# One kernel, one change: the depthwise convolution's work shared out anew in the first stage of a hybrid decoder trunk

## The chip, the cores and the metric

The kernel runs on one core of a Trainium2 chip. A core has five engines that run at the same time and in order, each from its own queue: TensorE (PE, matrix products, which write to a memory of eight banks called PSUM), VectorE (DVE), ScalarE (ACT), GpSimd (POOL) and SyncE (SP). SP and ACT also issue the DMA transfers here. The metric is the time of one execution on the device, in microseconds, and the median of several runs is compared. A profile comes from one further execution; its span runs from the first instruction to the last.

## The reference

Two layers on x of 512 tokens by 1024 channels, all in float32. Only the first half of the first layer is touched by the change:

```python
def conformer_conv(x, w_pw1, b_pw1, w_dw, b_dw, ln_g, ln_b, w_pw2, b_pw2):
    a = jax.nn.glu(x @ w_pw1 + b_pw1, axis=-1)
    y = lax.conv_general_dilated(          # causal, depthwise, 31 taps
        a, w_dw[:, None, :], window_strides=(1,),
        padding=((CONV_WIDTH - 1, 0),),
        dimension_numbers=('NWC', 'WIO', 'NWC'),
        feature_group_count=D_MODEL) + b_dw
    y = jax.nn.silu(layernorm(y, ln_g, ln_b))
    return y @ w_pw2 + b_pw2

h = h + conformer_conv(rmsnorm(h, norm_mix[0]), ...)
h = h + swiglu_ffn(rmsnorm(h, norm_ffn[0]), ffn_w_up[0], ffn_w_down[0])
# then: shared K/V, banded attention with a relative-position bias table,
# a second feed-forward part, and a final RMSNorm
```

## The kernel before

**Layout.** Activations lie with channels on the 128 partitions and the 512 tokens along the free axis, so the 1024 channels are eight tiles (ct = 0 to 7). Each float32 operand of a large product is split in a high part and a low rest (names `whi`, `wlo` for weights), and three matmuls (hi·hi, hi·lo, lo·hi) take the place of one. Weights arrive in chunks of 128 x 1024 (`raw`, 512 KB, on SP's queue). `advance` loads six chunks ahead and splits three ahead: a copy on ACT makes `whi`, a subtraction on DVE makes `wlo` (both line 269).

**Start.** x comes in four transfers on SP's queue (L375), the first weight chunk in three pieces on ACT's queue (L373), then on SP's queue the second chunk, `rnd` (a table of convolution weights, L378) and `wdw`. ACT and DVE split the eight tiles of x (each scaled by the norm's gain) and the first two chunks, in an order written out with `Turn`, a helper that puts every operation behind the one before (recorded at line 280). Then come the squares of x, whose sum gives the RMS scale. PE starts on the projection without that scale; the scale is multiplied in when the results are read out of PSUM.

**The RMS scale.** In the middle of tile 1's projection `step1` sums the squares over the partitions on PE. DVE then forms the mean square (L428), POOL takes it to the power -0.5 (L430), DVE writes it on diagonals (L442), and `step2` spreads it over all partitions with one product and a copy on ACT (L437, `rsbc`). Until then no projection result can be read out.

**A tile of the convolution.** `project` makes the linear and the gate half on PE, in an order written out by hand (`in_turn`, line 337). `gate` applies the RMS scale (L758, L760), the sigmoid on ACT (L759) and the product (L761) into `apad`, 512 tokens with 30 zeros in front. Then the 31 taps are shared out:

- *Rounds* on PE. `apad` is written to DRAM (`rowsd`, L766) and read back four times, shifted by one token each (`shifted`, L768), so that 32 channels times 4 shifts fill the partitions. A round applies four taps: four matmuls with 32 output channels each. Their weights, `tables`, are diagonals that DVE makes out of `eye` and `rnd` (L725).
- *Taps* on DVE: one fused multiply-add each (`taps`, recorded at 280), accumulated in a PSUM bank.
- *Products* on ACT (L803, L806) with the additions on POOL (L808, and L821 into y).
- On the last tile alone, four taps as full diagonal products on PE.

`ROUNDS`, `N_DIAG` and `N_DVE` set the shares; what remains goes to the products. `last` adds the rounds' bank to `y[ct]` (L825). The rounds of tile ct stand on PE inside the projection of tile ct + 2; those of tiles 4 to 7 stand behind all projections.

**LayerNorm.** `shift_rows` takes a common offset off y (two products with ones, L837). `sums` adds up y and y² for pairs of tiles on PE, in one bank. After the last tile `scales` copies that bank out, forms mean and variance per token, takes the power on POOL, and spreads both over the partitions (`pm`, `prs`). Then each tile is made: subtract, multiply (DVE), Silu (ACT, L935), a copy for the high part (L936) and a subtraction for the low part. They feed `pw2`, the second product.

**The bias table.** `table` makes one row of bias per head, `f1`. `table_rows` copies it in four transfers to 128 rows of DRAM (`fd`, L671), and `read_bias` reads it back along a diagonal, in eight transfers of two heads each (L957), during the second product; the attention needs it later.

`tc.issue_after` fixes that one instruction is put behind another; where nothing fixes it, the program's scheduler chooses the order on each engine. `held` gives the instructions behind which weight splits are put.

Of the kernel before, what the change touches and what calls it, by code (L numbers as in the profile page):

```python
# [37 lines left out]
ROUNDS = (3, 3, 3, 3, 3, 3, 4, 5)  # L38
N_DIAG = (0, 0, 0, 0, 0, 0, 0, 4)
N_DVE = (9, 9, 9, 9, 9, 9, 7, 4)  # L40
# [132 lines left out]
def hybrid_trunk(ctx: ExitStack, tc: tile.TileContext, xT, W, prm_in, wdw_in, rnd_in, sinks, relb, onehot, fin, out):  # L173
# [203 lines left out]
    rnd = cv.tile([P, ROUND_COLS[-1]], F32, tag="rnd", name="rnd", bufs=1)  # L377
    nc.sync.dma_start(rnd, rnd_in)  # L378
# [23 lines left out]
    class Rms:  # L402
# [16 lines left out]
        def step1(self):  # L419
# [8 lines left out]
            nc.vector.tensor_scalar(ms, st[:, 0:4], 1.0 / D, EPS, op0=ALU.mult, op1=ALU.add)  # L428
            self.rs = small.tile([P, 4], F32, tag="rs", name=uid("rs"))
            nc.gpsimd.tensor_tensor(self.rs, ms, mhalf, op=ALU.pow)  # L430
            self.diag = diagonals(self.rs)
# [212 lines left out]
    with conv_stage:  # L644
        sk = cpool.tile([P, NH], F32, tag="sk", name="sk")
        fd = dpool.tile([P, NH, 3 * P], F32, tag="fd", name="fd")
# [21 lines left out]
        def table_rows(n):  # L668

            rows = slice(n * 32, (n + 1) * 32)  # L670
            nc.sync.dma_start(fd[rows].rearrange("q h k -> q (h k)"), f1.to_broadcast([32, NH * 3 * P]))  # L671
# [12 lines left out]
        sel = cv.tile([P, 2], F32, tag="sel", name="sel", bufs=1)  # L684
# [7 lines left out]
        acts, dves = Turn(), Turn()  # L692
        for k in range(KT):
# [23 lines left out]
        begun = dves.last  # L717
        held[0] = (acts.last, dves.last)
        weights_of = {}
        for ct, r in enumerate(ROUNDS):  # L720
            at = ROUND_COLS[ct]
            t, base = (tables[0], 0) if ct < 5 else (tables[1], ROUND_COLS[5])
            weights_of[ct] = t[:, at - base:at - base + 4 * r, :]
            with tc.issue_after(begun):
                nc.vector.tensor_mul(weights_of[ct], eye.unsqueeze(1).to_broadcast([P, 4 * r, 32]),  # L725
                                     rnd[:, at:at + 4 * r].unsqueeze(2).to_broadcast([P, 4 * r, 32]))
        class Conv:
# [58 lines left out]
            def rounds(self):  # L786
# [3 lines left out]
                for n in range(self.r):  # L790
                    for g in range(4):
# [31 lines left out]
            def last(self):  # L823
                ct = self.ct
                nc.vector.tensor_add(y[ct], self.c, y[ct])  # L825
                if ct in (2, 3):
                    nc.gpsimd.tensor_add(y[ct], y[ct], shift)
# [443 lines left out]
```

## Time and profile before

| | |
|---|---|
| median of 3 runs | 1073.04 us (1072.49 to 1073.49) |
| the profiled execution | 1073.53 us |
| its span | 1071.6 us |
| mean granted PE clock | 0.989 |
| first stage, to the first matmul of the second product | 0 to 166.1 us |
| PE busy in the whole span | 1040.2 us (97%) |
| DVE, ACT, POOL busy | 764.5, 507.2, 199.0 us |

A row of the timeline gives the start and the length in us, the engine, the line, the operation with its output and inputs, and a count; in brackets the idle time of the engine ahead of it and what ended it. Float32 products show two records each, so "x24" at the rounds are twelve matmuls (three rounds). A row of the DMA issues gives the size of one transfer and the median time from issue to landing.

### The profile page before, as it was taken

How to read it: one execution, taken by the hardware profiler on the slowest of the kernel's cores; microseconds unless marked ns; L12 is line 12 of the kernel's file. 1: busy time of each engine (PE TensorE's matmuls, PEld its weight loads, DVE VectorE, ACT ScalarE, POOL GpSimd, SP SyncE). 2: the span in 40 equal slices, each digit the busy share in tenths (PEclk: the TensorE clock that was granted, in tenths of full speed). 3: DMA queues.
4: the chain of work that ended last, by engine and by line, in shares of the span. 5: the costliest groups of instructions: out<-in, count | busy, mean ns of one | idle time of the engine just before them, and what ended most of it. 6: DMA issues, size and time to landing. Idle time of an engine off the chain costs nothing.

```text
span 1071.6 us, 15899 instructions
## 1 busy us (share of the span) xinstructions
PE 1040.2 (97%) x6368; PEld 892.0 (83%) x6368; DVE 764.5 (71%) x988; ACT 507.2 (47%) x774; POOL 199.0 (19%) x209
## 2 busy tenths in 40 slices
PE   8888989999999999999999999999999999999997
PEld 6555727888999899899988777788899988998996
DVE  7869857769786577658576676577978755776663
ACT  6466645534354255235363675454445522552353
POOL 0698950321000000000022333132100000000000
PEclk9898999999999999999999999999999999999999
DMA  6767543324224124321322211232423341343112
GB/s 227 199 196 192 138 133 117 101 89 164 79 99 153 45 90 144 102 80 60 117 81 88 73 57 40 65 95 96 138 80 100 121 154 40 98 138 99 40 60 79
DMA packets 37205, 114.34 MB, mean 107 GB/s; under 512 B 4443, under 2 KB 7436, under 8 KB 37004
## 3 DMA queue, kind: packets, MB, share of 16 engines
q1 hardware_dynamic: 35836, 111.71, 33.3%
q10 hardware_dynamic: 1296, 1.62, 0.4%
q8 instruction: 50, 0.82, 0.3%
q14 instruction: 23, 0.19, 0.1%
HBM read 108.98 MB, written 7.49 MB: 109 GB/s over the span
## 4 chain that ended last, share of the span: by engine, by line
PE 81%; DVE 1%; issue 1%; ACT 1%; POOLq 0%; POOL 0%; ACTq 0%
PE bank L345 23%; PE bank L346 22%; PE bank L347 22%; PE bank L337 12%; PE bank L1200 2%; DVE quad L460 1%; DVE wlo L269 0%; PE bank L1190 0%; PE bank L452 0%; PE bank L426 0%; ACT whi L269 0%; DVE h L489 0%; ACT tmp L935 0%; ACT tmp L607 0%; ACT quad L459 0%
## 5 line engine op out<-in xcount | busy, mean ns | idle before, releaser
L346 PE MATMUL bank<-quad,whi 128*128 128x256 f32 (+1 forms) x1536 | 489.0, 320 | 0.9 <-DVE quad L460 0.9
L345 PE MATMUL bank<-quad,whi 128*128 128x256 f32 (+1 forms) x1536 | 482.9, 320 | 1.8 <-ACT quad L936 1.1
L347 PE MATMUL bank<-quad,wlo 128*128 128x256 f32 (+1 forms) x1536 | 481.9, 319 | 0.0
L269 ACT CAST whi<-raw 128x1024 fp32r<-128x1024 f32 x174 | 182.3, 1050 | 294.6 <-PE bank L346 195.2
L345 PEld LDWEIGHTS bank<-quad,whi 128*128 128x128 f32 x1536 | 291.2, 190 | 24.7 <-ACT quad L936 1.9
L346 PEld LDWEIGHTS bank<-quad,whi 128*128 128x128 f32 x1536 | 292.5, 190 | 22.7 <-DVE quad L460 1.3
L347 PEld LDWEIGHTS bank<-quad,wlo 128*128 128x128 f32 x1536 | 290.0, 190 | 20.6 <-issue 0.5
L269 DVE TENSOR_TENSOR wlo<-raw,whi 128x1024 fp32r<-128x1024 f32 x174 | 225.0, 1296 | 114.3 <-ACT whi L269 105.0
L337 PE MATMUL bank<-quad,whi 128*128 128x512 f32 x512 | 161.9, 397 | 2.4 <-ACT whi L280 2.4
L337 PEld LDWEIGHTS bank<-quad,whi 128*128 128x128 f32 x512 | 95.2, 189 | 29.2 <-issue 6.3
L269 DVE TENSOR_TENSOR wlo<-blocks,whi 128x1024 fp32r<-128x1024 f32 x54 | 65.4, 1221 | 57.0 <-ACT whi L269 57.0
L337 PE MATMUL bank<-quad,wlo 128*128 128x512 f32 x256 | 100.7, 393 | 2.1 <-DVE wlo L269 2.1
L269 ACT CAST whi<-blocks 128x1024 fp32r<-128x1024 f32 x54 | 56.6, 1048 | 91.6 <-PE bank L346 70.0
L808 POOL TENSOR_TENSOR quad<-quad 128x512 f32<-128x512 f32 x63 | 91.1, 1448 | 11.6 <-ACT quad L806 7.9
L337 PEld LDWEIGHTS bank<-quad,wlo 128*128 128x128 f32 x256 | 48.3, 189 | 13.5 <-DVE wlo L269 2.5
L1211 POOL TENSOR_TENSOR rs<-ss,mhalf 128x1 f32<-128x1 f32 x4 | 2.2, 548 | 297.9 <-DVE ss L1209 297.9
L806 ACT ACTIVATE quad<-apad,wdw 128x512 f32<-128x512 f32 x63 | 43.9, 719 | 26.4 <-POOL quad L808 26.2
L416 POOL TENSOR_TENSOR tmp<-tmp,tmp 128x512 f32<-128x512 f32 x21 | 33.0, 1571 | 113.0 <-ACT tmp L414 88.9
L1073 POOL COPY sc<-sk 128x4 f32<-128x4 f32 x16 | 3.5, 253 | 257.0 <-DVE wlo L269 254.8
L1097 POOL TENSOR_SCALAR sc<-sc,sm 128x256 f32<-128x256 f32 (+1 forms) x64 | 31.7, 515 | 67.5 <-DVE sm L1095 67.4
L489 DVE TENSOR_TENSOR h<-bank,h 128x512 f32<-128x512 f32 x56 | 37.1, 683 | 8.2 <-PE bank L347 8.1
L1093 ACT ACTIVATE sc<-sc,m 128x257 f32<-128x257 f32 (+1 forms) x64 | 30.2, 475 | 22.2 <-DVE m L1084 22.2
(158 smaller groups left out, 1007.2 us busy)
## 6 DMA issues: line engine op xcount, KB each, us to landing
raw<-in_W_dram SPq DMA_DIRECT2D x139, 512.0 KB, 3.5
blocks<-in_W_dram SPq DMA_DIRECT2D x36, 512.0 KB, 4.1
shifted<-rowsd SPq DMA_DIRECT2D x24, 260.0 KB, 5.6
fd<-f SPq DMA_DIRECT2D x4, 768.0 KB, 9.7
rowsd<-apad SPq DMA_DIRECT2D x8, 271.0 KB, 2.6
bias<-fd SPq DMA_DIRECT2D x8, 256.0 KB, 5.3
shifted<-rowsd SPq DMA_DIRECT2D x4, 264.0 KB, 5.1
shifted<-rowsd SPq DMA_DIRECT2D x4, 262.0 KB, 4.7
```

The lines of the kernel that those rows point to most:

```text
L269: done = (nc.scalar.copy(hi, r).ins, lo_engine[0].tensor_sub(lo, r, f32(hi)).ins)
L337: turn[0] = nc.tensor.matmul(*args, **kw).ins
L345: nc.tensor.matmul(out, w[0], x[0], start=start, stop=False, **kw)
L346: nc.tensor.matmul(out, w[0], x[1], start=False, stop=False, **kw)
L347: nc.tensor.matmul(out, w[1], x[0], start=False, stop=stop, **kw)
L416: eng.tensor_add(sq, self.acc[eng], sq)
L489: nc.vector.tensor_add(t, banks[m], t)
L806: nc.scalar.mul(pr, src, self.tap(j))
L808: nc.gpsimd.tensor_add(to, acc, pr)
L1093: nc.scalar.activation(sc[:, j, 0:1 + w], sc[:, j, 0:1 + w], AF.Exp, bias=self.m4[:, j:j + 1], scale=-1.0, accum_out=sm[:, j:j + 1])
L1097: nc.gpsimd.tensor_scalar(sc[:, j, 1:1 + w], sc[:, j, 1:1 + w], sm[:, j:j + 1], 0.0, op0=ALU.mult, op1=ALU.add)
L1200: nc.tensor.matmul(self.banks[g], x, w[:, k, :], start=False, stop=kp == LAST[1] - 1 and k == 1 and n == 2)
```

## The change

It has six parts, all in the first stage:

- **Shares.** Tiles 1, 3 and 5 get four rounds for three and eight DVE taps for nine; tile 6 gets eight taps for seven. Products per tile become 10, 7, 10, 7, 10, 7, 7, 3 (before 10 in tiles 0 to 5, then 8 and 3).
- **Order of the first loads.** `rnd` moves to ACT's queue behind the first quarter of the first weight chunk; x, the rest of that chunk and the second chunk go on SP's queue, in the order of use.
- **Tables.** Instead of eight together ahead of the mean square, three are made before all else on DVE, two behind the mean square (beside POOL's power), three behind the diagonals.
- **Bias table.** `fd` has 16 rows, one transfer, behind tile 3's projection; each of the eight reads then writes 16 partitions with all heads.
- **Offset.** `shift_rows` stands half a projection later, behind tile 4's.
- **LayerNorm.** The sums of tiles 4 to 6 and their copy (`means`) come ahead of tile 7's rounds. Tile 7's y is added in its PSUM bank by a product with the identity; its sums are eight products with a column of 1/1024, added onto the same bank. The first tile's high part is written by a Silu of its own.

```diff
-ROUNDS = (3, 3, 3, 3, 3, 3, 4, 5)
+ROUNDS = (3, 4, 3, 4, 3, 4, 4, 5)
-N_DVE = (9, 9, 9, 9, 9, 9, 7, 4)
+N_DVE = (9, 8, 9, 8, 9, 8, 8, 4)
...
-    for a, b in ((0, 256), (256, 512), (512, 1024)):
-        nc.scalar.dma_start(early[0][0][:, a:b], W[0][:, a:b])
-    for a, b in ((0, 1), (1, 2), (2, 4), (4, 8)):
+    nc.scalar.dma_start(early[0][0][:, 0:256], W[0][:, 0:256])
+    nc.scalar.dma_start(rnd, rnd_in)
+    load_x(0, 1)
+    load_x(1, 2)
+    nc.sync.dma_start(early[0][0][:, 256:1024], W[0][:, 256:1024])
+    load_x(2, 4)
     nc.sync.dma_start(early[1][0], W[1])
-    nc.sync.dma_start(rnd, rnd_in)
+    load_x(4, 6)
+    load_x(6, 8)
     nc.sync.dma_start(wdw, wdw_in)
...
             nc.gpsimd.tensor_tensor(self.rs, ms, mhalf, op=ALU.pow)
-            self.diag = diagonals(self.rs)
+            if between is not None:
+                had = between(had)
+            with tc.issue_after(had):
+                self.diag = diagonals(self.rs)
...
-        fd = dpool.tile([P, NH, 3 * P], F32, tag="fd", name="fd")
+        fd = dpool.tile([16, NH, 3 * P], F32, tag="fd", name="fd")
-            nc.sync.dma_start(fd[rows].rearrange("q h k -> q (h k)"), f1.to_broadcast([32, NH * 3 * P]))
+            nc.sync.dma_start(fd.rearrange("q h k -> q (h k)"), f1.to_broadcast([16, NH * 3 * P]))
...
+        def round_weights(cts, after=None):
+            for ct in cts:
+                at, n = ROUND_COLS[ct], 4 * ROUNDS[ct]
+                with tc.issue_after(after) if after is not None else nullcontext():
+                    after = nc.vector.tensor_mul(weights_of[ct], eye.unsqueeze(1).to_broadcast([P, n, 32]),
+                                                 rnd[:, at:at + n].unsqueeze(2).to_broadcast([P, n, 32])).ins
+            return after
+
+        dves.last = round_weights(range(3))
...
+                    if self.n_diag and n == self.r - 1:
+                        in_turn(self.c, ident, y[self.ct], start=False, stop=False, skip_group_check=True)
...
-        def scales():
+        def means():
             sc = temp()
-            with tc.issue_after(nc.scalar.copy(sc, st[0]).ins):
-                nc.scalar.activation(warm, warm, AF.Silu)
+            nc.scalar.copy(sc, st[0])
             b = bank()
             for n in range(NBLK):
-                in_turn(b[:, 2 * n:2 * n + 2], sc[:, n * P:(n + 1) * P], sel, start=True, stop=True)
+                in_turn(b[:, 2 * n:2 * n + 2], sc[:, n * P:(n + 1) * P], sel, start=n == 0, stop=False)
+            return b
+
+        def scales(b, c):
+            nc.vector.tensor_copy(y[KT - 1], c)
+            sq = next_of(1, sqs)
+            with tc.issue_after(nc.scalar.square(sq, c).ins):
+                nc.scalar.activation(warm, warm, AF.Silu)
+            for i, t in enumerate((y[KT - 1], sq)):
+                for n in range(NBLK):
+                    in_turn(b[:, 2 * n + i:2 * n + i + 1], t[:, n * P:(n + 1) * P], inv_d, start=False,
+                            stop=i == 1 and n == NBLK - 1)
...
-                    rms0.step1()
-                    held[0] = (spread_of[0],)
+                    rms0.step1(lambda after: round_weights((3, 4), after))
+                    held[0] = (round_weights((5, 6, 7), spread_of[0]),)
...
                 if half == 1 and n == 7:
                     if ct == 2:
                         table()
+                    if ct == 3:
+                        table_rows()
+                    if ct == 4:
+                        shift_rows()
...
-        held[0] = (tapped.last,)
+        held[0] = (tapped.last, convs[KT - 2].joined)
         advance()
         convs[KT - 1].diagonals()
+        sums(KT - 4, KT - 3)
+        sums(KT - 2)
+        b = means()
         convs[KT - 1].rounds()
-        convs[KT - 1].last()
-        sums(KT - 4)
-        sums(KT - 2)
-        idle(1)
-        pm, prs = scales()
+        pm, prs = scales(b, convs[KT - 1].c)
...
             if i == 0:
-                continue
+                act(nc.scalar.activation, z[i][0], t, AF.Silu, **ln)
+                act(nc.scalar.activation, t, t, AF.Silu, **ln)
+            else:
+                act(nc.scalar.activation, t, t, AF.Silu, **ln)
+                act(nc.scalar.copy, z[i][0], t)
...
-        for h0_ in range(0, NH, 2):
+        for p in range(0, P, 16):
             yield
-            nc.sync.dma_start(bias[:, h0_:h0_ + 2, :],
-                              bass.AP(tensor=fd.tensor, offset=fd.offset + 127 + h0_ * 3 * P,
-                                      ap=[[NH * 3 * P - 1, P], [3 * P, 2], [1, BAND]]))
+            nc.sync.dma_start(bias[p:p + 16, :, :],
+                              bass.AP(tensor=fd.tensor, offset=fd.offset + 127 - p,
+                                      ap=[[NH * 3 * P - 1, 16], [3 * P, NH], [1, BAND]]))
```

More of the change, by code (lines that the diff above doesn't have):

```diff
@@ L417, in add, with step1 @@
             self.acc[eng] = sq
-        def step1(self):
+        def step1(self, between=None):
             if self.stage:
@@ L840, in shift_rows, with sums @@
                 nc.vector.tensor_add(t, t, shift)
-        def sums(ct):
+            nc.gpsimd.tensor_add(y[2], y[2], shift)
+        def sums(*cts):
             if st[0] is None:
@@ L846, in sums @@
             src = []
-            for i in (ct, ct + 1):
+            for i in cts:
                 sq = next_of(1, sqs)
```

57 lines of the change are left out of this document (22 added, 35 removed).

## The prediction

> **What bounds the kernel now.** I read a table of stretches first, then each engine's timeline up to 170 us with the waits that it names, then the DMA issues.
>
> ```profile
> 22.50:45.40 22.90, 17.19 (x65) 12.31 (x64) 20.81 (x31) 10.01 (x15) 8.90 (x7) 0.85 0.58 173
> 45.40:74.00 28.60, 28.60 (x147) 19.54 (x148) 19.75 (x24) 16.92 (x25) 27.41 (x23) 1.00 0.56 166
> 74.00:83.50 9.50, 2.14 (x5) 0.50 (x4) 7.92 (x8) 6.21 (x10) 8.65 (x8) 0.79 1.02 282
> 83.50:131.28 47.78, 47.77 (x232) 33.24 (x233) 42.41 (x49) 31.02 (x45) 44.80 (x34) 0.97 0.60 157
> 166.10:1071.60 905.50, 897.24 (x5678) 802.01 (x5678) 637.48 (x825) 410.93 (x631) 89.91 (x116) 1.00 0.29 92
> ```
>
> Each table row gives its length, then busy time of PE, PEld, DVE, ACT and POOL, granted clock and DMA. From 166.1 us, where the second product of the convolution module begins, PE is busy 897.24 of 905.50 us. Nothing there is touched but eight DMAs, so what the first stage saves moves the end by as much. In the first stage PE is full from 45.40 to 74.00 and nearly so from 83.50 to 131.28. Its losses lie in four places: the RMS scale (22.5 to 45.4), the two waits around 74 to 83.5, the wait ahead of 148.4, and the LayerNorm chain after 154. POOL, although busy 44.80 of 47.78 us, does not hold PE there.
>
> **Part 1, the start and the RMS scale.**
>
> ```profile
> 4.73 0.75 DVE L280 SCALAR_TENSOR_TENSOR quad<-h,prm,quad 128x512 fp32r<-128x512 f32 x1 [2.42 <-ACT quad L280]
> 9.82 0.69 DVE L280 TENSOR_TENSOR wlo<-raw,whi 128x512 fp32r<-128x512 f32 x1 [1.40 <-ACT whi L280]
> 22.05 4.23 DVE L725 TENSOR_TENSOR tables<-eye,rnd 128x384 f32<-128x384 f32 x8
> 26.20 2.35 DVE L269 TENSOR_TENSOR wlo<-raw,whi 128x1024 fp32r<-128x1024 f32 x2
> 28.47 0.15 DVE L428 TENSOR_SCALAR ms<-bank 128x4 f32<-128x4 f32 x1
> 29.84 0.69 DVE L442 TENSOR_TENSOR tmp<-ident,rs 128x512 f32<-128x512 f32 x1 [1.22 <-POOL rs L430]
> 33.31 0.69 DVE L758 TENSOR_TENSOR tmp<-bank,rsbc 128x512 f32<-128x512 f32 x1 [0.52 <-ACT rsbc L437]
> ...
> 6.41 0.41 ACT L280 CAST whi<-raw 128x256 fp32r<-128x256 f32 x1 [0.40 <-DMA raw<-in_W_dram]
> ...
> 22.50 0.95 PE L337 MATMUL bank<-ones_c,tmp 128*128 128x1 f32 x8
> ...
> 45.40 2.78 PE L337 MATMUL bank<-shifted,tables 128*32 128x512 f32 x24 [1.99 <-DVE quad L280]
> ...
> rnd<-in_rnd_dram SPq DMA_DIRECT2D x1, 54.0 KB, 7.3
> shifted<-rowsd SPq DMA_DIRECT2D x2, 260.0 KB, 5.7
> ...
> 38.28 1.76 SPq L768 DMA_DIRECT2D shifted<-rowsd x4
> ...
> 174.56 1.13 PE bank L345 x5
> ```
>
> Now eight table products take DVE 4.23 us at 22.05, exactly where the mean square waits. The change puts three of them ahead of all else on DVE, two under POOL's power, three behind the diagonals. The first three wait for rnd, and every x part, weight split and sum on DVE now stands behind that wait. rnd takes the place of the second weight piece on ACT's queue. That piece (128 KB) had landed by 6.41; rnd is half as large. I take 5.8, then 1.6 us (three of eight, one larger), so DVE's first x part starts at 7.4, not 4.73. The old DVE waited for weights until 9.82 and ran dense from there; the 3.3 us of work before that point now end at 10.7, the rest of the inputs at 15.5 as before, because the joined queue brings the first weights earlier. PE loses about 1 us here, but reaches the sums (22.50, now 23.4) before DVE is ready anyway.
>
> Then DVE has two weight splits (2.35 us) from 22.05 and the mean square at 24.5: 4.0 earlier than 28.47. Two tables (1.15 us) fit beside POOL's power (1.22 us of waiting), so the diagonals also come 4.0 earlier, 25.8. Three tables (2.0 us) follow, in the 2.8 us ahead of the gate (33.31) that two more splits fill now; of those splits I let one still come ahead of the gate. Gate at 30.0 instead of 33.31: **3.3 earlier**. (None ahead: 4.4; both: 2.1.) Behind the gate lie the round trip through DRAM and the taps: the last shifted copy was issued at 39.6 (four in 1.76 us from 38.28) and took 5.7, so landed at 45.3, where the round matmuls start. That shifts to 42.0. PE, at five matmuls in 1.13 us, is there at 37.5 and waits 4.5 instead of 1.99.
>
> A wait that long has a price:
>
> ```profile
> 131.28 8.79 PE L337 MATMUL bank<-shifted,tables 128*32 128x512 f32 x80
> 140.00 3.70 PE L337 MATMUL bank<-apad,quad 128*128 128x512 f32 x8
> 148.40 5.82 PE L337 MATMUL bank<-shifted,tables 128*32 128x512 f32 x40 [4.69 <-DMA shifted<-rowsd]
> ```
>
> Ten rounds fill 131.28 to 140.00, 0.87 each; after the 4.69 us wait five take 5.82 instead of 4.4, 1.4 lost. After 1.99 us, three take 2.78: next to nothing. I take half, 0.7. Term: **-2.6 us**, bounds -4.4 and, with rnd as late as in its old place (landing after 11.7), +3.
> [...]
>
> **Part 2, between 45 and 131 us.**
>
> ```profile
> fd<-f SPq DMA_DIRECT2D x4, 768.0 KB, 9.7
> rowsd<-apad SPq DMA_DIRECT2D x1, 271.0 KB, 7.0
> rowsd<-apad SPq DMA_DIRECT2D x1, 271.0 KB, 2.6
> shifted<-rowsd SPq DMA_DIRECT2D x2, 260.0 KB, 9.0
> ...
> 77.90 1.12 PE L337 MATMUL bank<-quad,ones_m 128*128 128x512 f32 x2 [2.88 <-DVE quad L825]
> 83.51 4.12 PE L337 MATMUL bank<-shifted,tables 128*32 128x512 f32 x24 [4.49 <-DMA shifted<-rowsd]
> ```
>
> Four table copies of 768 KB flood SP's queue beside tile 2: its row copy lands in 7.0 us against 2.6 undisturbed, its shifted copies in 9.0 against 5.7. The new copy is 384 KB, once, behind tile 3's products. Without 7.7 us of delay tile 2 is there at about 75 by the old clock, ahead of PE, so the 4.49 goes, and the slow rounds after it (4.12 against 2.61): 1.5. The shift matmuls move behind 24 more matmuls (5.45 us), which covers the 2.88 wait for y[1]. Tiles 1 and 3 get a round each: +1.74. Sum: **-7.1 us**. Fewer products (71 to 61 on ACT, 63 to 53 adds on POOL) and two taps cost nothing and save nothing on PE by themselves; they keep the gates early:
>
> ```profile
> L808 POOL TENSOR_TENSOR quad<-quad 128x512 f32<-128x512 f32 x63 | 91.1, 1448 | 11.6 <-ACT quad L806 7.9
> 136.98 0.71 ACT L759 ACTIVATE tmp<-tmp,prm 128x512 f32<-128x512 f32 x1
> 132.00 0.68 DVE L758 TENSOR_TENSOR tmp<-bank,rsbc 128x512 f32<-128x512 f32 x1
> 137.72 0.75 DVE L761 SCALAR_TENSOR_TENSOR apad<-bank,prm,tmp 128x512 f32<-128x512 f32 x1 [4.43 <-ACT tmp L759]
> ```
>
> Ten adds at 1.448 take 14.5 us off POOL; PE comes only some 9.7 earlier, so POOL's lag, which holds back the last gate's sigmoid until 136.98, shrinks. If that cover is missing, PE waits for gates again: bound, half the term (-3.5). Other bound -8.5 (the 0.97 clock gone too).
>
> **Part 3, from the last projection (131.28) to the next product (166.10): 34.8 us now.**
>
> ```profile
> 159.25 0.16 DVE L280 COPY mv<-bank 128x4 f32<-128x4 f32 x1 [4.21 <-PE bank L337]
> 163.29 1.28 DVE L280 TENSOR_TENSOR tmp<-tmp,bank 128x512 f32<-128x512 f32 x2
> 164.02 1.52 ACT L935 ACTIVATE tmp<-tmp,prm 128x512 f32<-128x512 f32 x2 [4.50 <-DVE tmp L280]
> 166.10 1.20 PE L345 MATMUL bank<-quad,whi 128*128 128x512 f32 x4 [1.12 <-ACT quad L936]
> ```
>
> After: 11 rounds (9.6), diagonals (3.7), sums of tiles 4 to 6 (two times 0.9), the ACT copy that means() inserts, with PE idle behind it and tile 7's rounds queued behind PE (no row for it; nearest are the 512-column operations of 0.68 to 0.71 above, plus two handovers of 0.2: 1.1), its matmuls (0.5, half of the eight records at 22.50). That is 16.7 us. Without POOL's lag the last gate is written 2.9 us after the projection (0.7 handover, 0.68, 0.71, 0.75), and the row and shifted copies take another 9.8 (137.72 + 0.75 to 148.3 is that), so they land by 12.7: the 4.69 wait goes, with 4.0 us to spare. Then five rounds (4.4) and the identity product (0.9, as one of the four at 140.00): tile 7's taps complete at 21.9, against 22.9 now (148.40 + 5.82). Next, the copy and the square of the PSUM bank side by side (0.7), eight column matmuls (1.6 by the row at 22.50, 0.95 for four), handovers 0.35: mv at +2.65, where it is now +5.1. From mv to the first product with prs 4.04, unchanged. From there one DVE product and one Silu straight into the operand: 0.7 + 0.8 + 0.25 handovers, against 2.8 now; its low part comes some 0.5 us later than PE could use it. Sum 21.9 + 2.65 + 4.04 + 1.75 = 30.3: **-4.5 us**. Bounds: -1.5 if the shifted copies still come last; -6 if means() hides in some wait.
>
> The rest goes together at nothing: the memset for inv_d, the tables' other layout, y[2]'s shift on POOL. The splits for the second product now also wait for tile 6's sum. Behind them on DVE stand only tile 7's copy and the means; four splits (1.2 each in the row at 26.20, more beside POOL) start at 10.5 us after the projection and end by 18, ahead of 21.9. Without that cover the copy of tile 7 waits for what is left of them, at most 1.5.
>
> **Part 4, the eight bias DMAs** now write 16 partitions each.
>
> ```profile
> bias<-fd SPq DMA_DIRECT2D x8, 256.0 KB, 5.3
> 159.28 4.20 SPq L957 DMA_DIRECT2D bias<-fd x8
> 174.29 23.78 SPq L248 DMA_DIRECT2D raw<-in_W_dram x5
> shifted<-rowsd SPq DMA_DIRECT2D x1, 260.0 KB, 3.3
> ```
>
> I cost them at nothing: four weight chunks are in SBUF, and the fifth is needed four chunks of 5.45 us after 166.1, at 188. Taking off 6 for its own landing and split (an estimate from 5.3 and 1.2 above), the eight may hold the queue for 23 us from 159.3; they hold it about 10. A shifted copy onto 32 partitions landed in 3.3, so 16 partitions should stay near that.
> [...]
>
> **Sum.** -2.6 - 7.1 - 4.5 = -14.2. The profiled run was 1073.53 (span 1071.6 and 1.9 around it), 0.5 above the median 1073.04; span 1057.4, and about **1059 us** against the median.
>
> **Rivals.** (a) The start goes wrong: rnd late on a shared queue, or both splits ahead of the gate, or the tail keeps its shifted wait. Then -2.6 becomes 0 to +3, or -4.5 becomes -1.5: 1062 to 1067, say 1064. For it: DVE's very first work now hangs on one small DMA. Against: the second weight piece landed by 6.41. (b) No split ahead of the gate, no slow clock, means() hidden: -4.4 - 8.5 - 6, about 1054. (c) The change doesn't do what it says: PE's waits at 78 and 83 were only where POOL's and ACT's lag showed, and return at another round; with the three added rounds (2.6) nothing much is left, 1071 to 1075. For: POOL busy 44.80 of 47.78. Against: PE never waited in that stretch. (d) Slower: the bias writes. At half the rate of the 260 KB in 3.3 us, eight take 52 us; beyond 23 PE starves in the second product: 29 - 14 = +15, 1088. It decides from about 2.9 us each in a row. Against: same packets of 1 KB, same 2 MB.
>
> **How the numbers follow.** Forecast 0.54 (own range 1056 to 1062), (a) 0.22, (b) 0.12, (c) 0.06, (d) 0.06. Faster is taken as over 0.2% (2.1 us, about what a measurement of this kernel can tell from no change): 0.88; same 0.06; slower 0.06. The range 1053 to 1067 takes in (a) and (b) and leaves out (c), (d) and their edges.
>
> **What would show it.** Right: rnd landed before 6.5; mean square near 24.5; first gate near 30; no wait for shifted copies after the first tile; the shift sums without a wait; mv within 3 us of the last round; the second product starting near 152. Wrong: DVE idle beyond 8 us at the start; the mean square again behind splits; a wait for shifted copies at 145; weight DMAs after 174 held behind bias.

## The result, and the profile after

The changed kernel takes **1068.16 us** (median of 5 runs, 1065.23 to 1068.47) against 1073.0 for the kernel before, a ratio of 0.9949 with the interval 0.9934 to 0.9965. It is faster, by 4.8 us. The forecast was 1059 with a range of 1053 to 1067: the sign was right, a gain of 14 was not there, and the time lies 1.2 us above the range. The profiled execution took 1066.32 us. Of all runs named below, one of e9's four took 5855 us and is left out; every other counts.

Below is the table of stretches of the changed kernel: length, busy time of PE, PEld, DVE, ACT and POOL, granted PE clock, DMA share and GB/s. The cuts are the start of the sums of squares, the end of tile 0's rounds, the start of tile 2's rounds, the end of the last projection and the first matmul of the second product.

```profile
24.94:52.37 27.43, 19.59 (x90) 12.43 (x88) 23.62 (x33) 14.41 (x20) 15.93 (x14) 0.82 0.72 192
52.37:79.28 26.91, 26.91 (x130) 18.96 (x130) 20.81 (x23) 16.68 (x23) 22.59 (x18) 0.99 0.47 135
79.28:128.33 49.05, 49.05 (x245) 33.92 (x245) 43.05 (x50) 31.48 (x48) 45.90 (x35) 1.00 0.65 158
128.33:160.79 32.46, 30.85 (x185) 10.97 (x184) 15.70 (x23) 8.37 (x14) 6.63 (x6) 0.95 0.55 128
160.79:1064.50 903.71, 895.75 (x5679) 800.51 (x5678) 638.02 (x826) 412.56 (x633) 89.72 (x116) 1.00 0.31 94
```

The same cuts in the kernel before:

```profile
48.18:131.28 83.10, 75.73 (x359) 52.43 (x359) 67.40 (x77) 52.65 (x76) 78.24 (x61) 0.96 0.63 172
131.28:166.10 34.82, 28.12 (x166) 9.22 (x165) 20.58 (x27) 14.88 (x25) 18.19 (x12) 0.95 0.59 169
```

The middle went from 83.10 to 75.96 us (26.91 + 49.05), and PE is busy in all of it. The tail went from 34.82 to 32.46. But the first stretch, to the end of tile 0's rounds, grew from 48.18 to 52.37, with the clock at 0.82. PE's timeline shows where:

```profile
8.53 0.79 PE L337 MATMUL bank<-quad,whi 128*128 128x512 f32 x1 [2.65 <-DVE quad L280]
...
24.94 0.95 PE L337 MATMUL bank<-ones_c,tmp 128*128 128x1 f32 x8
...
47.02 5.35 PE L337 MATMUL bank<-shifted,tables 128*32 128x512 f32 x24 [7.83 <-DMA shifted<-rowsd]
...
137.91 3.70 PE L337 MATMUL bank<-apad,quad 128*128 128x512 f32 x8
141.54 2.85 PE L337 MATMUL bank<-quad,ones_m 128*32 128x512 f32 x12
145.07 1.05 PE L337 MATMUL bank<-sel,tmp 128*128 128x2 f32 x8 [0.68 <-ACT tmp L882]
146.05 3.64 PE L337 MATMUL bank<-shifted,tables 128*32 128x512 f32 x32
149.62 1.12 PE L337 MATMUL bank<-quad,ident 128*128 128x512 f32 x2
150.68 1.07 PE L337 MATMUL bank<-shifted,tables 128*32 128x512 f32 x8
152.63 1.95 PE L337 MATMUL bank<-sel,quad 128*128 128x1 f32 x16 [0.88 <-DVE quad L890]
...
160.79 1.20 PE L345 MATMUL bank<-quad,whi 128*128 128x512 f32 x4
```

PE loses 2.65 us at its second product, reaches the sums of squares 2.4 us later than before (24.94 for 22.50), stands for 7.83 us ahead of tile 0's rounds, and then needs 5.35 us for what took 2.78. All waits for copies after that are gone. Between the diagonals (137.91) and the second product two waits stand, 0.68 and 0.88 us. DVE's timeline says what came ahead of tile 0's gate, which begins with L774 and ends with the product into `apad` (L777):

```profile
6.18 1.63 DVE L712 TENSOR_TENSOR tables<-eye,rnd 128x384 f32<-128x384 f32 x3 [3.89 <-DMA rnd<-in_rnd_dram]
...
25.92 0.16 DVE L435 TENSOR_SCALAR ms<-bank 128x4 f32<-128x4 f32 x1 [1.29 <-PE bank L337]
...
28.22 2.02 DVE L712 TENSOR_TENSOR tables<-eye,rnd 128x512 f32<-128x512 f32 x3
30.16 2.35 DVE L269 TENSOR_TENSOR wlo<-raw,whi 128x1024 fp32r<-128x1024 f32 x2
32.43 0.68 DVE L774 TENSOR_TENSOR tmp<-bank,rsbc 128x512 f32<-128x512 f32 x1
33.03 0.69 DVE L776 TENSOR_TENSOR bank<-bank,rsbc 128x512 f32<-128x512 f32 x1
33.63 0.68 DVE L774 TENSOR_TENSOR tmp<-bank,rsbc 128x512 f32<-128x512 f32 x1
34.23 0.69 DVE L776 TENSOR_TENSOR bank<-bank,rsbc 128x512 f32<-128x512 f32 x1
34.82 0.74 DVE L777 SCALAR_TENSOR_TENSOR apad<-bank,prm,tmp 128x512 f32<-128x512 f32 x1
```

The mean square comes 2.5 us earlier than the 28.47 of before, but now it waits for PE. Behind the diagonals stand three tables and two weight splits, so tile 0's gate begins at 32.43 (33.31 before). Tile 1's L774 and L776 come between, and the product into `apad` stands at 34.82, where it stood at 34.79 before: the 2.5 us are gone. SP's queue then puts a weight chunk and tile 1's row copy in front of tile 0's shifted copies, and tile 1's shifted copies right behind them:

```profile
35.64 0.33 SPq L782 DMA_DIRECT2D rowsd<-apad  x1
36.72 0.33 SPq L248 DMA_DIRECT2D raw<-in_W_dram  x1
37.42 0.33 SPq L782 DMA_DIRECT2D rowsd<-apad  x1
38.52 5.70 SPq L784 DMA_DIRECT2D shifted<-rowsd  x8
```

Tile 0's shifted copies are issued from 38.52 on, against 38.28 before, but the last of the four lands 7.0 us after its issue, against 5.7.

The DMA issues (KB each, median us to landing) that the prediction spoke of:

```profile
bias<-fd SPq DMA_DIRECT2D x8, 256.0 KB, 10.2
...
rnd<-in_rnd_dram ACTq DMA_DIRECT2D x1, 60.0 KB, 4.4
```

`rnd`, issued at 1.65, landed near 6.1, a little later than the 5.8 that was taken. The bias writes take nearly twice the 5.3 us of before, and nothing waits for them.

### The profile page after: what moved, and what is told of

It is laid out like the page before. It is cut to its first block, busy times and chain, and to the rows that moved or that the text cites. A ratio compares the mean times of both kernels' runs of the same rounds, so it can differ in the third digit from the quotient of the medians.

```text
span 1064.5 us, 15933 instructions
## 1 busy us (share of the span) xinstructions
PE 1042.4 (98%) x6404; PEld 893.5 (84%) x6404; DVE 759.7 (71%) x986; ACT 500.7 (47%) x764; POOL 182.0 (17%) x200
## 4 chain that ended last, share of the span: by engine, by line
PE 94%; DVE 2%; DMA 1%; issue 1%; ACT 1%; POOL 0%; SPq 0%; POOLq 0%; ACTq 0%; DVEq 0%
PE bank L337 24%; PE bank L345 23%; PE bank L346 23%; PE bank L347 22%; PE bank L1226 2%; DVE quad L470 1%; DMA shifted<-rowsd 1%; DVE wlo L269 0%; DMA rnd<-in_rnd_dram 0%; DVE tables L712 0%; DMA rowsd<-apad 0%; PE bank L1216 0%; PE bank L462 0%; PE bank L433 0%; ACT whi L269 0%
## 5 line engine op out<-in xcount | busy, mean ns | idle before, releaser
L269 DVE TENSOR_TENSOR wlo<-raw,whi 128x1024 fp32r<-128x1024 f32 x174 | 221.3, 1275 | 110.7 <-ACT whi L269 99.6
L826 POOL TENSOR_TENSOR quad<-quad 128x512 f32<-128x512 f32 x53 | 72.9, 1376 | 19.1 <-ACT quad L824 15.9
L824 ACT ACTIVATE quad<-apad,wdw 128x512 f32<-128x512 f32 x53 | 36.6, 717 | 17.2 <-POOL quad L826 17.2
## 6 DMA issues: line engine op xcount, KB each, us to landing
bias<-fd SPq DMA_DIRECT2D x8, 256.0 KB, 10.2
```

What stands on the lines that cost most here:

```text
L269: done = (nc.scalar.copy(hi, r).ins, lo_engine[0].tensor_sub(lo, r, f32(hi)).ins)
L824: nc.scalar.mul(pr, src, self.tap(j))
L826: nc.gpsimd.tensor_add(to, acc, pr)
```

## The experiments

The theory after these traces had three parts. (A) The start costs about 4 us: DVE's first work hangs on `rnd`, and DVE's and SP's order ahead of the first copies costs as much again. (B) The tail earns 2.3. (C) The middle earns 7 because the table no longer floods SP's queue. The rival for (C): the waits in the middle were slack behind POOL, and the shares earn what is earned. Ratios stand against runs of the kernel before taken beside each experiment, with 95% intervals. By an interval of 0.003 one ratio is known to about 1.6 us on either side.

### The start: e1 to e6

**e1** puts tile 0's gate on DVE ahead of the last three tables, the splits and tile 1's gate:

```diff
-                nc.vector.tensor_mul(sig, self.gt, rs_bc)
+                with tc.issue_after(convs[0].gated) if ct == 1 else nullcontext():
+                    nc.vector.tensor_mul(sig, self.gt, rs_bc)
...
-                    held[0] = (round_weights((5, 6, 7), spread_of[0]),)
+                    split_limit[0] = 5
...
-                    convs[0].begin()
+                    convs[0].gate()
+                    held[0] = (round_weights((5, 6, 7), convs[0].gated),)
...
```

> Tile 0's gate goes on DVE ahead of the last three tables, of the two weight splits and of tile 1's gate; nothing else moves. Theory A (the start's gain was lost on DVE, in the order of what stands between the diagonals and the first gate): the first gate is written near 32.5 us instead of 35.6, tile 0's last shifted copy lands near 44 instead of 47, PE's wait of 7.8 us shrinks to about 5, and the median falls by 3 to 4 us to about 1064.5. Theory B (the copies were late because of the traffic on SP's queue, wherever the gate stands): they land at 46 or later and the median stays at 1067 to 1068.

Measured: 1066.51, ratio 0.9934 (0.9917 to 0.9951). In its profile the product into `apad` follows the sums of squares by 6.8 us (34.52 after 27.68) where the change needs 9.9. But the sums came 2.7 us later here: `rnd` took 5.8 us to land instead of 4.4, and PE needed 17.76 us instead of 16.41 from its second product to the sums. Tile 0's rounds still ended 4.7 us earlier than in the change (47.66), at a granted clock of 1.00 (38 to 52 us). Then tile 2's rounds waited 4.13 us for their copies and took 5.35 instead of 2.78, and the gain was lost there.

**e2** leaves DVE alone and puts tile 1's row copy and the weight chunk on SP's queue behind tile 0's shifted copies:

```diff
-                nc.sync.dma_start(ad, a)
+                with tc.issue_after(convs[0].sent) if ct == 1 else nullcontext():
+                    nc.sync.dma_start(ad, a)
...
```

> On SP's queue tile 1's row copy and the weight chunk that were issued ahead of tile 0's shifted copies are put behind them; DVE's order stays. Theory B: tile 0's row copy is written at 35.6 as in the change, its shifted copies land 9.7 us later, near 45.3 as in the kernel before, 1.7 earlier than in the change; median about 1066. Theory A by itself: the queue does little, landing between 46 and 47, median 1067 to 1068.

Measured: 1066.37, 0.9941 (0.9926 to 0.9956). In its profile PE no longer waits for tile 0's copies, but for DVE's taps, 6.71 us. **e3** does both.

> Both of the two edits above. If A and B both hold they add: gate at 32.5, copies landing near 42, PE's wait down to 3 us, the rounds behind it at full clock (2.8 us instead of 5.4): 7 us less, median about 1061. If something else holds tile 0's rounds (the PSUM bank of its DVE taps), PE's wait goes over to DVE and no more than 3 us are gained.

Measured: 1065.17, 0.9931 (0.9916 to 0.9945). The wait ahead of tile 0's rounds fell to 3.12, but the weight chunks got ahead of tile 1's row copy (44.29 for 37.42), and tile 2's rounds then waited 2.33 us for their own copies. None of the three differs from the change by more than the intervals allow.

**e4** has 24 products more, whose result nothing uses, ahead of tile 0's rounds, to keep PE's clock up.

```diff
+                if ct == 2 and half == 0 and n == 7:
+                    t = bank()
+                    for _ in range(24):
+                        in_turn(t, x[0][0][:, 0:P], x[0][0], start=True, stop=True)
```

> Twenty-four more products of a 128x512 operand (their result is not used) stand on PE ahead of tile 0's rounds, 5.5 us of work in a wait of 7.8. Theory C (part of the loss at the start is PE's clock, which falls in the long wait): the three rounds take 2.8 us instead of 5.35 and the median falls by about 2.5 us, to 1065.5. If the slow rounds have another cause, they stay at 5.3 and the median at 1068.

Measured: 1067.61, 0.9942 (0.9923 to 0.9961), no gain. The rounds took 4.22 instead of 5.35: PE still waited 2.50 us behind the added products.

**e5** moves the first three tables behind the second x part on DVE:

```diff
-        dves.last = round_weights(range(3))
...
+            if k == 1:
+                dves.last = round_weights(range(3), dves.last)
```

> The change, with the first three table products moved on DVE from ahead of all x parts to behind the second one; nothing else. Theory D (the wait of DVE's first work for rnd costs PE a stall of 2.5 to 4 us and a cold clock behind it, and the varying landing of rnd is what spreads the runs): PE's wait for the first x part goes, the sums of squares start at 22.5 to 22.8 us instead of 24.9 to 27.7, the runs lie closer together, and the median falls by 2 to 3 us to about 1065.5. Rival: the delay is hidden, because tile 0's rounds wait for the gate's order on DVE and for the copies anyway; then the sums come earlier and the median stays near 1068.

Measured: 1065.89, 0.9927 (0.991 to 0.9944). PE's first wait went and the sums of squares started at 22.53, but PE then stood 9.31 us ahead of tile 0's rounds: what the start gains, the wait for the copies takes. **e6** is e5 with e1's order on DVE, and on SP tile 0's copies, then tile 1's row copy, then weights.

> e5's edit and the two edits of e3 together, with tile 1's row copy directly behind tile 0's shifted copies and the weight chunks behind it. If the losses at the start are DVE's start (D), DVE's order ahead of the gate (A) and the queue (B), one behind the other, all are gone: first gate near 30 us, tile 0's rounds near 41, full clock; the predicted -2.6 of part 1 and more, median 1059 to 1061. If another limit stands behind them (DVE's taps, by their PSUM bank), tile 0's rounds start at 43 or later and the median is 1063 or more.

Measured: 1062.57, 0.9897 (0.9882 to 0.9912), about 5.6 us better than the change. DVE's and PE's timelines of e6, one row of DVE and then two of PE (line numbers differ by a few between the kernels):

```profile
29.96 0.75 DVE L782 SCALAR_TENSOR_TENSOR apad<-bank,prm,tmp 128x512 f32<-128x512 f32 x1 [0.19 <-ACT tmp L779]
```

```profile
40.18 4.48 PE L339 MATMUL bank<-shifted,tables 128*32 128x512 f32 x24 [2.79 <-DVE bank L282]
...
73.53 4.40 PE L339 MATMUL bank<-shifted,tables 128*32 128x512 f32 x24 [2.06 <-DVE bank L781]
```

With PE early, the gate begins at 28.47 and its product into `apad` stands at 29.96, 4.9 us ahead of the change; the rounds start at 40.18, 6.8 us ahead. So (A) holds: no part of it alone gains more than the 2.4 us of e5 by its ratio, and together they gain 5.6. What e5 gained ahead of the gate PE waited for at tile 0's copies; what e1 and e3 gained at tile 0 was lost, wholly or in part, at tile 2.

### The middle: table or shares, e7, e8, e10, e13

**e7** is the kernel before with the 16-row table, its reads and the later offset, and nothing else; **e8** is the change with `ROUNDS` and `N_DVE` of before; **e10** is the kernel before with the new shares alone; **e13** is e7 and e10 together.

```diff
-ROUNDS = (3, 3, 3, 3, 3, 3, 4, 5)
+ROUNDS = (3, 4, 3, 4, 3, 4, 4, 5)
-N_DVE = (9, 9, 9, 9, 9, 9, 7, 4)
+N_DVE = (9, 8, 9, 8, 9, 8, 8, 4)
...
-        fd = dpool.tile([P, NH, 3 * P], F32, tag="fd", name="fd")
+        fd = dpool.tile([16, NH, 3 * P], F32, tag="fd", name="fd")
...
```

> The kernel before, with only the table copied to 16 rows in one transfer behind tile 3's projection, the bias read as in the change, and the offset taken half a projection later. Part 2 of the prediction by itself, without the rounds: the waits of 2.88 and 4.49 us and the slow rounds go, 8 to 9 us less, median about 1064 to 1065. If POOL's lag sets the gates, the wait comes back at another tile and less than 4 us are gained.

> The change with the shares of before (rounds, taps and products). The prediction took the three added rounds as 2.6 us of PE time that keep the gates early. If the cover is needed: the last gate's sigmoid lags again, PE waits for tile 7's copies by 2 us or more, and the median is the same as the change's or above it. If it isn't needed: PE saves 2.6 us and the median falls to about 1065.5.

Measured: e7 1072.75, 0.9995 (0.9985 to 1.0004), nothing; e8 1071.63, 0.9981 (0.9967 to 0.9994). PE's timeline of e7, the last gate on its DVE, and ACT ahead of that gate's sigmoid (L757):

```profile
78.14 2.78 PE L337 MATMUL bank<-shifted,tables 128*32 128x512 f32 x24 [1.81 <-DMA shifted<-rowsd]
...
136.09 3.64 PE L337 MATMUL bank<-shifted,tables 128*32 128x512 f32 x32 [2.86 <-DMA shifted<-rowsd]
...
148.56 6.11 PE L337 MATMUL bank<-shifted,tables 128*32 128x512 f32 x40 [5.20 <-DMA shifted<-rowsd]
```

```profile
138.07 0.75 DVE L759 SCALAR_TENSOR_TENSOR apad<-bank,prm,tmp 128x512 f32<-128x512 f32 x1 [4.38 <-ACT tmp L757]
```

```profile
136.71 0.72 ACT L804 ACTIVATE quad<-apad,wdw 128x512 f32<-128x512 f32 x1 [0.63 <-POOL quad L806]
137.33 0.71 ACT L757 ACTIVATE tmp<-tmp,prm 128x512 f32<-128x512 f32 x1
```

The waits of 2.88 and 4.49 at 78 and 83 shrank to 1.81. But a new wait of 2.86 stands ahead of tile 6's rounds, and the 4.69 ahead of tile 7's grew to 5.20, because the last gate stands at 138.07 where it stood at 137.72: ACT's sigmoid comes behind products that wait for POOL's chain of additions, and that chain is as long as before (its last addition ends at 149.04 in e7 and at 148.69 before). In this profile the middle falls from 83.10 to 77.46 and the tail grows from 34.82 to 38.69; tile 0's rounds, slow here, take 1.7 more. The rival looked right here, and so the shares were tried alone.

> The kernel before with one part of the change, the shares: a round more for tiles 1, 3 and 5, a product less on VectorE for each of these, hence fewer products and adds on GpSimd (the table keeps its four copies). If GpSimd's chain of products set the last gates, that gate (137.7 before) comes several us earlier and the waits ahead of tiles 6 and 7 go, while the waits at 78 and 83 stay and PE pays 2.6 us for three rounds: in all 2 to 4 us gained, 1069 to 1071 for 1073. By the prediction (fewer products save nothing on PE by themselves): 2.6 lost, 1075 to 1076.

> The kernel before with two parts of the change, the shares (e10) and the table copied once onto 16 rows (e7), with start and tail as before. Alone the shares gave 5.2 us and the table nothing. If GpSimd's lag was all that stood behind the table's waits, the two together remove the waits ahead of tile 2 (5.7 us in e10's profile) and its slow rounds (1.6) without a new wait: about 7 us below e10, 1060 to 1061. If something else is late in that place (the y joins on VectorE, the split of the products), the sum stays near e10: 1066 to 1067. If the latter, what e9 (1064.2) gained over the change lies in the start, not in the tail.

Measured: e10 **1067.47**, 0.9950 (0.9933 to 0.9967): the shares alone are worth as much as the whole change, more than was expected. e13 **1061.62**, 0.9892 (0.9877 to 0.9908): the table, worth nothing by itself, adds some 6 us to them. Tile 2's rounds in e10, where in e13 they start at 76.87 after a wait of 1.00:

```profile
83.24 4.41 PE L337 MATMUL bank<-shifted,tables 128*32 128x512 f32 x24 [5.72 <-DMA shifted<-rowsd]
```

The stretches of e10 (middle and tail), then of e13:

```profile
48.98:132.15 83.17, 77.45 (x376) 53.05 (x375) 65.31 (x76) 51.41 (x75) 73.18 (x58) 0.96 0.68 180
132.15:161.75 29.60, 27.59 (x173) 9.06 (x173) 17.82 (x24) 9.51 (x16) 6.97 (x5) 1.00 0.58 177
```

```profile
49.06:125.90 76.84, 75.84 (x375) 52.82 (x374) 64.71 (x75) 47.92 (x68) 69.62 (x54) 1.00 0.60 153
125.90:155.51 29.61, 27.60 (x174) 9.07 (x173) 19.95 (x26) 12.22 (x22) 13.45 (x8) 1.00 0.68 158
```

The shares leave the middle at 83.17, where tile 2's copies are still late, and take the tail from 34.82 to 29.60, since the last gate is early (133.05) and no wait for copies is left there. The table then takes the middle to 76.84. Each removes one of two delays in a row. Without the shares, the second delay returns most of what the table saves (3.9 of 5.6 us in e7's profile).

### The tail: e9

**e9** is the change with the LayerNorm of before (tile 7's y joined on DVE, sums of tiles 4, 5 and of 6, 7 behind tile 7's rounds).

```diff
-        sums(KT - 4, KT - 3)
-        sums(KT - 2)
-        b = means()
         convs[KT - 1].rounds()
-        pm, prs = scales(b, convs[KT - 1].c)
+        convs[KT - 1].last()
+        sums(KT - 4, KT - 3)
+        sums(KT - 2, KT - 1)
+        idle(1)
+        pm, prs = scales()
...
```

> The change with the LayerNorm tail of before: tile 7's tap sum joined on VectorE, sums of tiles 4, 5 and of 6, 7, the old scales and the old order of the normalised tiles. It prices part 3 alone. By the two profiles the new tail is worth 2.3 us of 34.8 (32.5 against 34.8), so 1070.5 for the change's 1068.2. By the prediction's part 3 it is worth 4.5: 1072.7. If what the tail saves is hidden in front of it (the last tile's copies come last either way), nothing: 1068.

Measured: 1063.75, the median of three, 0.9915 (0.9899 to 0.9932). All three expectations missed: by the ratios the change is faster by 3.6 us without its new tail. So (B) is wrong. PE's timeline of e9:

```profile
129.27 9.65 PE L337 MATMUL bank<-shifted,tables 128*32 128x512 f32 x88
...
142.48 4.50 PE L337 MATMUL bank<-shifted,tables 128*32 128x512 f32 x40
146.80 4.41 PE L337 MATMUL bank<-quad,ones_m 128*32 128x512 f32 x18
...
158.87 1.20 PE L345 MATMUL bank<-quad,whi 128*128 128x512 f32 x4 [1.12 <-ACT quad L953]
```

From 129.27 to 158.87 are 29.60 us, as in e10, against 32.46 in the change. The copies for tile 7 are there when PE comes (142.48, no wait), so there is nothing to fill ahead of its rounds. The old order runs them at once and sums tiles 4 to 6 while DVE and ACT make tile 7's y and its square. The new order spends that cover first (2.85), then waits 0.68 and 0.88 with nothing else to do, and adds 1.12 for the identity and 1.95 for sixteen column records.

### Without what costs: e11, e12, e14

**e11** is e6 with the table copy behind tile 2's shifted copies on SP (in e6 it stood ahead of tile 2's row copy). **e12** is e11 with tile 6's sums behind tile 7's second round and the means behind the fourth. **e14** is e11 with e9's tail.

```diff
-            nc.sync.dma_start(fd.rearrange("q h k -> q (h k)"), f1.to_broadcast([16, NH * 3 * P]))
+            with tc.issue_after(convs[2].sent):
+                nc.sync.dma_start(fd.rearrange("q h k -> q (h k)"), f1.to_broadcast([16, NH * 3 * P]))
```

> e6_start_gate with the one table copy on SyncE's queue behind tile 2's shifted copies instead of ahead of tile 2's row copy. In e6 the copy stood at 60.35, tile 2's row copy at 61.64, and tile 2's rounds waited 2.06 us and then took 4.40 instead of 2.78. If the copy is what delays tile 2, both go: about 3 us less, 1059 to 1060 for 1062.6. If what holds tile 2 is its gate or GpSimd's share, it stays at 1062.6.

> e11_fd_late with the tail in another order on PE: tile 6's sums after tile 7's second round and the means' products after its fourth, so that ScalarE's square and copy lie beside rounds. In the change's profile tile 7's rounds stood behind 1.8 us of waiting (tile 6's square, then the copy of the means). If tile 7's shifted copies have landed by then, about 1.7 us less than e11: near 1058. If they come last (they landed 9.8 us behind the last gate in the kernel before), the wait only moves: as e11.

> e11_fd_late with the tail of before in place of the new one. In the profiles the old tail takes 29.6 us from the last projection to the second product (e9 and e10) and the new one 32.5 (the change), so 2.9 less than e11: 1058. If the old tail is short only because of what its own kernel left earlier (the last gate, the clock), 1061 as e11. e12 (the new tail in another order) has 1059.1.

Measured: e11 1060.93, 0.9887 (0.9868 to 0.9906); e12 1059.08, 0.9868 (0.9853 to 0.9883); e14 **1056.83**, 0.9846 (0.9832 to 0.986). e11 is inconclusive: in its profile tile 2's rounds still waited 2.11 us, for a weight split on DVE, and its interval overlaps that of e6. e12 can't be told from e11 either. e14's interval lies below that of e11, so the old tail is better than the new one here too; against e12's order of the new tail the intervals still overlap. e14 beats both kernels, the one before by 16.5 us. Its middle and tail:

```profile
44.73:121.38 76.65, 75.86 (x376) 52.81 (x375) 69.03 (x80) 47.35 (x68) 69.38 (x54) 1.00 0.65 168
121.38:151.94 30.56, 27.64 (x174) 9.37 (x173) 21.25 (x28) 13.58 (x23) 14.77 (x9) 1.00 0.72 165
```

## Why the prediction was right in sign and wrong in size

The change can be built up in four steps, each a kernel that ran. In us: the end of tile 0's rounds, the middle to the end of the last projection, the tail to the second product, the rest of the span, and the ratio.

| | to round 0's end | middle | tail | rest | ratio |
|---|---|---|---|---|---|
| before | 48.18 | 83.10 | 34.82 | 905.50 | 1 |
| + shares (e10) | 48.98 | 83.17 | **29.60** | 903.25 | 0.9950 |
| + table (e13) | 49.06 | **76.84** | 29.61 | 904.59 | 0.9892 |
| + start (e9) | **53.20** | 76.07 | 29.60 | 903.13 | 0.9915 |
| + tail = the change | 52.37 | 75.96 | **32.46** | 903.71 | 0.9949 |

The rest, where little but the bias transfers differs, still varies by 2.4 us between these profiles, so the columns of one profile don't add up to the ratio exactly. Two parts earn about 11.6 us together (1 - 0.9892, of 1073) and two give 6 back. The intervals of e13 and e9 overlap, so the start's loss rests on the profiles (4.1 at the end of the rounds) and on e6 more than on that step's ratio. Those of e9 and the change don't.

**Part 1, -2.6 predicted, +4.2 measured: the step that failed first.** The prediction said of the start: "PE loses about 1 us here, but reaches the sums (22.50, now 23.4) before DVE is ready anyway". PE stood for 2.65 us, then worked at a granted clock of 0.90 up to the sums, which came at 24.94, and the mean square (25.92 for 24.5) waited for them. It said "of those splits I let one still come ahead of the gate": two came, and tile 1's two products that nobody had counted. So the gate began at 32.43 instead of 30.0, and its product into `apad` stood at 34.82 instead of 31.5 (30.0 and the 1.48 from L758 to L761 before). The prediction moved the copies as a block with the gate, while the rounds follow that product by 12.20 us instead of 10.61. And the clock took 2.57 (5.35 for 2.78, at a granted 0.50 from 47.02 to 52.37) where 0.7 was taken. These three, 3.3, 1.6 and 1.9, are the 6.8 between -2.6 and +4.2. e6 mends the orders on DVE and on SP's queue: its gate begins 1.5 us ahead of the 30.0 forecast and its rounds 1.8 ahead of the 42.0. The step was possible, but the change left its order open.

**Part 2, -7.1 predicted, -7.1 measured.** The size held, and so did the reason: the waits go because the flood goes (e10 to e13), and they stay gone only because the shares shorten POOL's chain (e7). The prediction named that condition, as the cover that keeps the gates early, but priced its absence too low: half the term was to be left (-3.5), and e7 gains nothing by its ratio. That the fewer products "save nothing on PE by themselves" is wrong as it stands: alone the shares gave 5.4 us of 1073, in the tail, where the prediction booked the lost wait under part 3. Rival (c), 1071 to 1075 with waits that return at another round, describes e7 and also e8 (1071.63), the change without the shares. It failed for the change because the shares were in it. The one copy that is left did not stand behind tile 3's projection, as was meant: SP's queue has it at 62.00, ahead of tile 2's row copy (63.67) and of tile 1's rounds (64.61), which lie inside that projection. Tile 2 wasn't late even so. Added rounds and fewer products weren't tried apart, nor the 16 rows and the later offset.

**Part 3, -4.5 predicted, -2.4 measured: the step that failed second.** That "the 4.69 wait goes" was right, but it is the shares that remove it, with the old tail as well (29.60). What the sum of 30.3 never did was to work out the old tail without its wait. Compared with that, the prediction's own new tail would have lost 0.7, and the measured one loses 2.9. The 2.2 between 30.3 and 32.46 are mis-sized terms. The sums of tiles 4 to 6 took 2.85 for two times 0.9, as tile 6's square starts only at 142.67 and PE's last weight load stands behind it at 143.35; the means' products took 1.05 for 0.5, since the eight records at 22.50 are the four products already; mv followed the last round by 2.86 for 2.65; and the spread took about 0.5 longer than its 4.04, at a granted clock of 0.50 from 156 to 158 us. By the tables of stretches the tail's granted clock is 0.95 in the change, 0.91 in e8, 0.90 in e11 and 0.94 in e12, all with the new tail, and 1.00 in e9, e10, e13 and e14, with the old one; in the kernel before and e7, where PE stands 4.69 and 5.20 us ahead of tile 7's rounds, it is 0.95 and 0.96. With the old shares the new order did fit: there tile 7's copies come late, and by the table of stretches the tail takes 36.58 us in e8 against 38.69 in e7.

**Part 4, nothing predicted, nothing measured.** The bias writes landed in 10.2 us instead of 5.3. They were issued from 154.64 in 3.84 us, the first landed after 4.5 us and the last 17.6 us after its issue, near 175.6. The next weight chunk was issued at 169.83, and PE did not wait. In the table of stretches DMA moved 114 GB/s from 154.64 to 174.00:

```profile
154.64:174.00 19.36, 18.93 (x65) 12.22 (x65) 16.62 (x28) 11.15 (x16) 1.41 (x1) 0.91 1.09 114
```

At that rate 2 MB take 18.4 us.

Against the list of signs: `rnd` before 6.5, no wait for copies after the first tile, the shift sums without a wait and mv within 3 us came as written; the mean square (25.92 for 24.5), the gate (32.43 for 30) and the second product (160.79 for 152) did not.

## What to carry to other kernels

Where two engines hold the same work up one behind the other, a part that frees only one of them can measure as nothing, and its partner as all: try the parts alone and together before dropping either. When a wait goes, work out the old order without it before pricing a new order that was made to fill it. Of an operation that is moved to the front, count what the first engine in the chain now waits for, and whatever the scheduler is free to put between.

## What the runs showed of the hardware

**Tile 0's rounds ran slow after a wait of 1.96 us and at full clock after one of 3.02.** PE's timelines of e7 and e11:

```profile
45.93 4.48 PE L337 MATMUL bank<-shifted,tables 128*32 128x512 f32 x24 [1.96 <-DVE quad L280]
```

```profile
40.15 2.78 PE L339 MATMUL bank<-shifted,tables 128*32 128x512 f32 x24 [3.02 <-DVE bank L282]
```

After 1.96 us the rounds took 4.48 us, after 3.02 they took 2.78: the length of the wait alone did not tell. In the traces of the two kernels the changes of the granted clock, full to half and back, lie whole multiples of 3.41 us apart; between 20 and 160 us they stand at 28.23, 35.06, 79.43, 86.26, 147.70 and 151.11 us in the kernel before (2, 13, 2, 18 and 1 times 3.41), at 42.55, 52.79, 155.19 and 158.60 in the change (3, 30 and 1 times). The tables of stretches of e7 and e11, cut in steps of that length:

```profile
42.62:46.04 3.42, 1.46 (x10) 0.91 (x13) 3.31 (x6) 1.44 (x2) 3.26 (x3) 1.00 1.06 282
46.04:49.45 3.41, 3.41 (x20) 1.09 (x21) 3.27 (x5) 1.61 (x3) 3.17 (x4) 0.50 0.78 231
```

```profile
35.57:38.98 3.41, 1.56 (x7) 0.94 (x6) 3.41 (x4) 1.45 (x2) 3.25 (x3) 1.00 0.93 185
38.98:42.39 3.41, 2.24 (x24) 0.81 (x24) 3.34 (x6) 1.31 (x2) 3.25 (x3) 1.00 0.40 95
```

e7's wait lies within one step, of which PE is idle for 57%, and the next step is granted 0.50. e11's wait is shared by two steps, idle for 54 and 34%, and the clock stays at 1.00. The same tables of the kernel before, then of the change, each with a step at full clock and what follows it:

```profile
24.82:28.23 3.41, 1.36 (x6) 0.83 (x5) 3.41 (x5) 1.03 (x1) 0.00 (x0) 1.00 0.00 0
28.23:35.06 6.83, 5.16 (x11) 2.86 (x10) 4.91 (x8) 1.31 (x2) 1.03 (x1) 0.50 0.75 251
41.88:45.30 3.42, 1.53 (x7) 0.94 (x5) 3.31 (x6) 1.30 (x3) 3.26 (x3) 1.00 1.01 266
45.30:48.71 3.41, 3.31 (x27) 1.31 (x28) 3.27 (x5) 1.75 (x3) 3.25 (x3) 1.00 0.76 239
76.02:79.43 3.41, 1.12 (x2) 0.30 (x2) 3.23 (x5) 0.95 (x2) 3.31 (x4) 1.00 0.97 258
79.43:86.26 6.83, 2.75 (x16) 0.89 (x20) 6.47 (x8) 5.62 (x9) 6.00 (x6) 0.50 0.96 277
```

```profile
39.13:42.55 3.42, 0.05 (x1) 0.00 (x0) 3.28 (x5) 1.53 (x4) 3.22 (x3) 1.00 1.01 333
42.55:52.79 10.24, 5.78 (x25) 1.62 (x26) 7.67 (x11) 5.66 (x8) 9.89 (x9) 0.50 0.84 168
151.77:155.19 3.42, 2.56 (x18) 2.08 (x18) 1.20 (x5) 2.08 (x3) 0.00 (x0) 1.00 0.00 0
155.19:158.60 3.41, 3.36 (x5) 1.09 (x5) 1.94 (x3) 0.00 (x0) 1.41 (x1) 0.50 0.94 131
```

Between 20 and 140 us of these two profiles, half the clock followed the three steps at full clock of which PE was idle for 60, 67 and 99%, and no other at full clock; the next idlest was idle for 55%. Behind the column records of the change's tail it followed a step idle for only 25%. What lowers the clock is not shown.

**The later `rnd` landed, the later the sums of squares started, in five profiles of six.** `rnd`, 60 KB, landed 4.4 us after issue in the change's profile and 4.8, 5.0, 5.5 and 5.8 in those of e9, e2, e3 and e1; the sums of squares started at 24.94, 25.60, 26.42, 26.50 and 27.68. (e4, with 4.7 and 25.81, is out of this order.) Where DVE doesn't begin with it (e5, e6, e14) they start at 22.53, 22.77 and 22.65. That this makes the times of the change vary from run to run (by 3.2 us) is not shown: e6's vary by 2.9 us without it, and those of 19 runs of the kernel before by 4.5.
